# A hybrid mixer block: gates and branch projections token-major, SSD heads in alternating halves, and another lane order at the start

## Chip, cores and metric

One core of one Trainium2 chip. The metric is the device time of one execution in microseconds, median of three runs: 2150.59 (2144.82 to 2153.54). All data are float32; the large matmuls split each operand into two float32r parts (hi and lo) and add three products.

## What is computed

One layer of a diffusion transformer over 256 tokens of width 2048. The inputs x and ctx are normed and modulated, projected by a wide w_in, and run through four branches (gated depthwise convolution, SSD scan, Fourier mixing, RWKV-7 scan). Each branch is projected to width 2048, weighted by a sigmoid gate of its own, and summed; then come w_o, a residual and a squared-ReLU MLP. Cut to what the change touches:

```python
def gated_merge(gate_pre, branches, w_o):
    gates = jax.nn.sigmoid(gate_pre).reshape(b, l, N_BRANCH, D_MODEL)   # gate_pre = h @ w_in[:, 5976:], 4 x 2048 columns
    m = gates[:, :, 0] * branches[0]
    for i in range(1, N_BRANCH):
        m = m + gates[:, :, i] * branches[i]                            # branches[i] = features @ out_i
    return m @ w_o

# ssd_scan, for each of 12 heads (64 wide), two directions, chunks of 128:
y_diag = jnp.einsum('bgrcls,bcsgrp->bclgrp', CB[:, :, None] * L, xd)
y_off = jnp.einsum('bclgn,bcgrpn->bclgrp', Cc, states[:, :-1]) * jnp.exp(a_cs)[..., None]
# modulation: mod = silu(c) @ mod_w + mod_b  (2048 x 12288), split into sh1, sc1, g1, sh2, sc2, g2
# conformer branch: a depthwise convolution of 31 taps over 512 channels
```

## The kernel before

The kernel is written in a tile framework that orders each engine's instructions by a simulated timeline; a number handed to `high_priority` moves a piece of work forward or back in that order. The big matmuls are the main stream. Beside them run lanes: generators that the main stream advances by `step(us)`. Each `next` of a lane emits a few instructions and yields its own estimate; a lane's rate says how much of its estimate it may emit for each microsecond that the main stream claims, and its offs is its priority.

Stages in order. `startup` loads x and ctx, computes the modulation columns it needs from mod_w (`modblock`, 64 loads of 512 KB in buffers "mw", MW of them; its matmuls are 32 wide and go to four 32-partition groups in turn), and runs the first w_in columns (`startcols`). `mid1` and `mid2` run the other columns of w_in in blocks of 512. Behind mid1's first blocks start the lane `rwkv` (RATE_RWKV, ROFF; its pieces a, A, b, c are weighted by WT, its buffers "x2" are XB) and `mod_lane` (rates MR), which computes the other four modulation vectors on VectorE: a load "rm" of 128x512 of mod_w, MB = 3 in flight, and a multiply-add into "macc" (line 1455). Both `mw` and `rm` loads are issued by SyncE (SP), whose queue is in order. `mid2` goes through the conv, Fourier and SSD columns and then the sixteen gate blocks (loop `for b in range(16)`). The lane `taps` (RATE_TAPS, TOFF) does the 31-tap convolution on VectorE (line 1180) in tiles "vp" and "cv" of the pool "mo", which lives through the whole kernel. When the RWKV pieces are far enough, `mid2` starts the lane `ssd` (RATE_SIDE, SOFF), and when RWKV is done, `fft` and `conv` (RATE_CONV, COFF).

Every weight unit of 2 x 128 x 512 is loaded (`unit`, line 155), cast to hi on ScalarE (line 166) and its rest taken to lo on VectorE (line 167), for each half of 128x512. `mm3` (lines 178 to 180) issues the three products. `block` is feature-major: the weights are the stationary operand, 128 columns at a time, the 256 tokens of h are the moving one, so the output is [feature, token], and one k-tile of 512 columns takes 4 x 3 matmuls of 256 columns. `rowblock` is token-major: 128 tokens of h are stationary, 512 weight columns move, and one k-tile takes 2 x 3 matmuls of 512 columns. The Fourier columns, w_o and the MLP's down projection use `rowblock`; the gate blocks, through `cols`, use `block`.

A gate block ends with a Tanh of each of two PSUM tiles (line 603) into "gs" and a store to DRAM "gd". `outs` goes through the branches in the order rwkv, fft, conv (4 k-tiles each), ssd (6): for each of four blocks of 512 output columns it loads two gate tiles "gt" (line 1530), multiplies, and merges the result into m (lines 1551 to 1554), all feature-major, as `hsplit` and w_o need it.

In `ssd`, each head makes an operand G and an operand Ce in buffers "s2" (S2 = 11) and issues four float32 matmuls of 64 stationary columns (lines 1407 and 1409) into half of a PSUM tile `py`: even heads in partitions 0 to 63, odd ones in 64 to 127. `py` is taken at the even head and read after the odd one. A float32 matmul shows as two records in the trace, a transpose and a float32r matmul as one.

Of the kernel before, what the change touches and what calls it, by code (L numbers as in the profile page):

```python
# [10 lines left out]
P = 128  # L11
OFFS = 100
RATE_RWKV = 1.4
RATE_SIDE = .508
RATE_CONV = .279
AHEAD = 2
S2 = 11
ROFF = 100
SOFF = 100
S1 = 14  # L20
WT = dict(a=1.0, A=.813, b=.999, c=.72)
MR = .26, .26, .109, .244
HB = 5
B4 = 8
COFF = -100
MB = 3
XB = 8
MW = 6
RATE_TAPS = .183
# [6 lines left out]
D = 2048  # L36
# [57 lines left out]
class K:  # L94
# [95 lines left out]
    def run(self):  # L190
        from contextlib import ExitStack
        nc, tc, io = self.nc, self.tc, self.io
        with ExitStack() as es:
# [4 lines left out]
            eh, eg, em, ep, er, ex, ed, ec = [ExitStack() for _ in range(8)]  # L198
# [14 lines left out]
            self.mrate = MR[0]  # L213
            self.rb, self.rx = pool(er, "rb", side="right"), pool(ex, "rx", side="right")
# [3 lines left out]
            ec.close()  # L218
            with ExitStack() as e1:
                self.outs(pool(e1, "o1", side="right"))  # L220
# [46 lines left out]
    def modblock(self, c0, w):  # L267


        nc = self.nc  # L270
        ps = self.psm()[:, :w]
        ke = 1024 // w
        st = max(4, ke)
        for u in range(0, KT, st):
            ws = []
            for k in range(u, u + st, ke):
                raw = self.t(self.sp, "mw", [P, 1024], bufs=MW).rearrange("p (t c) -> p t c", t=ke)
                nc.sync.dma_start(raw, self.wap(self.io["mod_w"][0], k, ke, c0, w))  # L278
# [309 lines left out]
    def mid2(self, prep, er, open_ssd, open_side):  # L588
# [11 lines left out]
        def gate(b):  # L600
            def evac(i, ps):
                o = self.GS()
                nc.scalar.activation(o, ps, AF.Tanh, scale=0.5)
                nc.sync.dma_start(self.g_d[2 * b + i], o)
            return evac
# [8 lines left out]
        for b in range(16):  # L614
            cols(C_G + 512 * b, gate(b))
# [547 lines left out]
    def taps(self):  # L1163
# [4 lines left out]
        for f in range(4):  # L1168
            vp = self.t(self.mo, "vp", [P, 4, 94], bufs=1)
# [3 lines left out]
            cv = self.t(self.mo, "cv", [P, TOK], bufs=1)  # L1173
# [82 lines left out]
    def ssd(self):  # L1256
# [66 lines left out]
        py = None  # L1323
        for hf in range(2):
# [11 lines left out]
            for gl in range(2):  # L1336
# [30 lines left out]
                for hl in range(3):  # L1367
# [33 lines left out]
                    yield 2.5  # L1401
                    if h % 2 == 0:
                        py = self.psm()
                    o = py[64 * (h % 2):64 * (h % 2) + 64, :TOK]
                    xo = (192 * gl + 64 * hl)
                    for i in range(2):
                        nc.tensor.matmul(o, xtk[:, 2 + i, xo:xo + 64], G[:, i], start=i == 0, stop=False)
                    for d in range(2):
                        nc.tensor.matmul(o, S0[:, d, 64 * hl:64 * hl + 64], Ce[:, d], start=False, stop=d == 1)
# [22 lines left out]
    def mod_lane(self):  # L1432
# [4 lines left out]
        for which in (2, 4, 3, 5):  # L1437
# [4 lines left out]
            for j in range(4):  # L1442
                acc = self.t(self.mo, "macc", [P, 512])
                for kt in range(KT):
                    while len(ahead) < MB and todo:
                        w2, j2, k2 = todo.pop(0)
                        raw = self.t(self.mo, "rm", [P, 512], bufs=MB)
                        nc.sync.dma_start(raw, io["mod_w"][0][k2 * P:(k2 + 1) * P, w2 * D + 512 * j2:w2 * D + 512 * j2 + 512])
                        ahead.append(raw)
# [59 lines left out]
    def outs(self, op):  # L1509
# [3 lines left out]
        for n in ("rwkv", "fft", "conv", "ssd"):  # L1513
# [13 lines left out]
            for b in range(4):  # L1527
                gt = [self.t(op, "gt", [P, 512], bufs=4) for _ in range(2)]
                for i in range(2):
                    nc.sync.dma_start(gt[i], self.g_d[(gi * 16 + b * 4) // 2 + i])  # L1530
                acc = [self.t(self.pa, "acc", [P, 512]) for _ in range(2)]
                for u in range(k // 2):
                    wu = self.unit([(self.wap(io[wname][0], 2 * u, 2, 512 * b, 512), 0)], 2, 512)
                    for f in range(4):
                        for i in range(2):
                            kt = 2 * u + i
                            c = (f % 2) * TOK
                            self.mm3(acc[f // 2][:, c:c + TOK], (wu[i][0][:, f * P:f * P + P], wu[i][1][:, f * P:f * P + P]),
                                     F[kt], u == 0 and i == 0 and f % 2 == 0,
                                     u == k // 2 - 1 and i == 1)  # L1540
                    self.step(2.4)
# [6 lines left out]
                for i in range(2):  # L1548
                    m, om = half(self.m[b], i), half(old, i)
                    if first:  # L1550
                        nc.vector.scalar_tensor_tensor(m, gt[i], 1.0, acc[i], op0=ALU.add, op1=ALU.mult)
                    else:
                        nc.vector.scalar_tensor_tensor(gt[i], gt[i], 1.0, acc[i], op0=ALU.add, op1=ALU.mult)
                        (nc.vector if n == "ssd" else nc.gpsimd).tensor_tensor(m, om, gt[i], op=ALU.add)
            first = False
        self.hx = ([], [])
        for b in range(4):
            self.hsplit(self.hx, self.m[b], self.p0)
# [184 lines left out]
```

## Time and profile before

| | |
|---|---|
| median of three runs | 2150.59 us |
| the profiled execution | 2151.65 us, of it a span of 2149.9 |
| TensorE, its records' share of the span | 96% |
| VectorE, ScalarE, GpSimd | 70%, 48%, 12% |
| bytes moved | 450.99 MB, mean 210 GB/s |

The trace is one execution. Times are from the span's start. A matmul's record is longer than the distance to the next one's start, since matmuls are pipelined and their ends are modelled: what one costs in a stream is read from starts.

### The profile page before, as it was taken

Reading aid. Unit: us, or ns where it says so; the run is one execution under the profiler, and the core shown is the slowest. Engines: PE = TensorE matmul, PEld = TensorE weight load, DVE = VectorE, ACT = ScalarE, POOL = GpSimd, SP = SyncE. Lnnn points to the kernel's source line nnn. Section 1 sums busy time; section 2 is a strip of 40 time slices with the busy share of each in tenths; the row PEclk is TensorE's granted clock in tenths of the full one; section 3 lists DMA queues with packets and bytes.
Section 4 is the critical chain, followed back from the end, with each engine's and each line's share of the span. In section 5 each row is a group of like instructions: output and inputs, shape, how many; then the busy total and the mean of one; then the engine's idle time right before and its main releaser. Section 6 shows DMA issues by size and latency. Waiting matters only on the chain.

```text
span 2149.9 us, 39741 instructions
## 1 busy us (share of the span) xinstructions
PE 2058.0 (96%) x14894; PEld 1884.8 (88%) x14894; DVE 1503.0 (70%) x2699; ACT 1022.7 (48%) x1934; POOL 251.9 (12%) x285
## 2 busy tenths in 40 slices
PE   6999999999999999899999999999999999999997
PEld 5758999998989999798888998899998889999886
DVE  5645875679999779587987787565766655555555
ACT  4212443454654554355666645464554444545443
POOL 1001430022131022021221140000000000000001
PEclk9999999999999999899999999999999999999999
DMA  9983636767666765579876677546867666666554
GB/s 337 318 273 106 186 87 203 234 165 219 197 187 201 214 185 167 177 219 299 265 247 197 205 270 263 188 124 184 262 205 271 234 210 185 185 185 192 192 194 157
DMA packets 310828, 450.99 MB, mean 210 GB/s; under 512 B 70969, under 2 KB 116700, under 8 KB 310124
## 3 DMA queue, kind: packets, MB, share of 16 engines
q1 hardware_dynamic: 308716, 441.86, 65.9%
q10 hardware_dynamic: 1472, 6.49, 0.9%
q8 instruction: 117, 1.92, 0.4%
q14 instruction: 75, 0.61, 0.1%
q0 software_dynamic: 448, 0.11, 0.0%
HBM read 424.22 MB, written 24.16 MB: 209 GB/s over the span
## 4 chain that ended last, share of the span: by engine, by line
PE 71%; DVE 11%; DMA 10%; issue 3%; SPq 2%; ACT 1%; POOL 1%; DVEq 0%; ACTq 0%; POOLq 0%
PE acc L180 20%; PE acc L179 20%; PE acc L178 20%; DMA rm<-in_mod_w 3%; DVE lo L167 2%; DMA raw<-in_w_in 2%; PE sm L282 2%; DVE macc L1455 2%; PE sm L1009 1%; DMA t<-scrA 1%; ACT hi L166 1%; DMA scrA<-x 1%; DMA raw<-in_fourier_out 1%; DVE tm L800 1%; SPq L278 1%
## 5 line engine op out<-in xcount | busy, mean ns | idle before, releaser
L167 DVE TENSOR_TENSOR lo<-raw,hi 128x512 fp32r<-128x512 f32 x1096 | 760.8, 712 | 434.4 <-ACT hi L166 414.6
L166 ACT CAST hi<-raw 128x512 fp32r<-128x512 f32 x1096 | 651.6, 617 | 800.0 <-PE acc L179 442.6
L180 PE MATMUL acc<-h,lo 128*128 128x256 f32 x3056 | 861.6, 286 | 16.1 <-DVE lo L167 15.8
L178 PE MATMUL acc<-h,hi 128*128 128x256 f32 x3056 | 865.7, 286 | 7.7 <-ACT hi L166 5.0
L179 PE MATMUL acc<-h,hi 128*128 128x256 f32 x3056 | 864.7, 285 | 1.5 <-DVE h L173 1.5
L180 PEld LDWEIGHTS acc<-h,lo 128*128 128x128 f32 x3056 | 575.2, 190 | 31.0 <-DVE lo L167 21.4
L178 PEld LDWEIGHTS acc<-h,hi 128*128 128x128 f32 x3056 | 578.4, 190 | 27.0 <-issue 11.8
L179 PEld LDWEIGHTS acc<-h,hi 128*128 128x128 f32 x3056 | 580.0, 190 | 16.4 <-issue 13.4
L1455 DVE SCALAR_TENSOR_TENSOR macc<-rm,sct,macc 128x512 f32<-128x512 f32 x240 | 193.1, 805 | 68.4 <-DMA rm<-in_mod_w 66.9
L179 PE MATMUL acc<-lo,uh 128*128 128x512 f32 x512 | 200.1, 391 | 0.0
L180 PE MATMUL acc<-hi,ul 128*128 128x512 f32 x512 | 199.3, 389 | 0.0
L178 PE MATMUL acc<-hi,uh 128*128 128x512 f32 x512 | 179.0, 389 | 0.0
L178 PEld LDWEIGHTS acc<-hi,uh 128*128 128x128 f32 x512 | 96.1, 188 | 19.9
L179 PEld LDWEIGHTS acc<-lo,uh 128*128 128x128 f32 x512 | 96.1, 188 | 19.9 <-DVE lo L167 0.2
L180 PEld LDWEIGHTS acc<-hi,ul 128*128 128x128 f32 x512 | 96.1, 188 | 19.8
L1689 POOL TENSOR_TENSOR yg<-yg,grow 128x512 f32<-128x512 f32 x8 | 10.9, 1368 | 721.5 <-ACT junk L1688 721.5
L179 PE MATMUL acc<-lo,h 128*128 128x512 f32 x160 | 63.9, 399 | 1.6 <-DVE lo L167 1.6
L180 PE MATMUL acc<-hi,h 128*128 128x512 f32 x160 | 63.3, 396 | 0.0
L1180 DVE SCALAR_TENSOR_TENSOR cv<-vp,col,cv 128x256 f32<-128x256 f32 x120 | 62.7, 523 | 0.4
L472 DVE TENSOR_TENSOR ua<-acc,ua 128x512 f32<-128x512 f32 (+1 forms) x50 | 34.0, 687 | 38.9 <-PE acc L180 38.6
L178 PE MATMUL acc<-hi,h 128*128 128x512 f32 x160 | 57.5, 396 | 1.1 <-ACT hi L166 1.1
L282 PE MATMUL sm<-mw,s 128*32 128x256 f32 (+2 forms) x448 | 57.0, 450 | 0.0
(379 smaller groups left out, 2476.7 us busy)
## 6 DMA issues: line engine op xcount, KB each, us to landing
raw<-in_w_in SPq DMA_DIRECT2D x216, 512.0 KB, 4.5
rm<-in_mod_w SPq DMA_DIRECT2D x256, 256.0 KB, 3.6
raw<-in_mlp_up SPq DMA_DIRECT2D x128, 512.0 KB, 3.6
raw<-in_mlp_down SPq DMA_DIRECT2D x128, 512.0 KB, 4.0
mw<-in_mod_w SPq DMA_DIRECT2D x64, 512.0 KB, 6.1
raw<-in_w_o SPq DMA_DIRECT2D x32, 512.0 KB, 3.6
gd<-gs SPq DMA_DIRECT2D x32, 256.0 KB, 4.3
gt<-gd SPq DMA_DIRECT2D x32, 256.0 KB, 3.4
```

Of the source, the lines that this page charges most:

```text
L166: nc.scalar.copy(b, a)
L167: nc.vector.tensor_tensor(c, a, b.bitcast(F32), op=ALU.subtract)
L178: nc.tensor.matmul(out, w[0], x[0], start=st, stop=False, skip_group_check=True)
L179: nc.tensor.matmul(out, w[0], x[1], start=False, stop=False, skip_group_check=True)
L180: nc.tensor.matmul(out, w[1], x[0], start=False, stop=sp, skip_group_check=True)
L278: nc.sync.dma_start(raw, self.wap(self.io["mod_w"][0], k, ke, c0, w))
L282: nc.tensor.matmul(ps[32 * j:32 * j + 32, :], self.s32[:, u + i, :], ws[i], start=u + i < 4, stop=u + i >= KT - 4, skip_group_check=True)
L472: nc.vector.tensor_tensor(ua[:m], ps[:m], ua[:m], op=ALU.add)
L800: nc.vector.tensor_tensor(o, Y[:, :r, u:u + 1].broadcast_to([P, r, n]), U[:, u:u + 1, u + 1:].broadcast_to([P, r, n]), op=ALU.mult)
L1009: nc.tensor.matmul(ch(ps, i), self.tb[n][d][:, i], ch(v, i), start=True, stop=True)
L1180: nc.vector.scalar_tensor_tensor(o, v, w, o, op0=ALU.mult, op1=ALU.add)
L1455: nc.vector.scalar_tensor_tensor(acc, raw, w, acc, op0=ALU.mult, op1=ALU.add)
```

## The change

The gate blocks run through `rowblock`, so gates are stored token-major: [token, column]. The projections of the branches in `outs` do the same, and the merged m is token-major. Because w_o needs m feature-major, a new function `mcols` transposes each block of m on TensorE (eight transposes of 128x128 a block) and splits it from PSUM; blocks 0 to 2 are done one SSD block later, block 3 at the end. In `ssd` an even head keeps its operand pairs, and the odd head issues all eight matmuls, alternating between the two halves of `py`. mod_lane's loads are placed behind the last mod_w load of the startup on their queue. "vp" and "cv" move to a pool "tp" that is open only in the middle. Startup has seven "mw" buffers in place of six, RWKV seven "x2" in place of eight, and rates, weights and priorities of the lanes have other values.

```diff
-RATE_RWKV = 1.4
-RATE_SIDE = .508
-RATE_CONV = .279
+RATE_RWKV = 1.451
+RATE_SIDE = 0.69
+RATE_CONV = 0.28
-ROFF = 100
-SOFF = 100
+ROFF = 68
+SOFF = 30
-WT = dict(a=1.0, A=.813, b=.999, c=.72)
-MR = .26, .26, .109, .244
+WT = {'a': 1.0, 'A': 0.728, 'b': 1.021, 'c': 0.887}
+MR = (0.26, 0.264, 0.109, 0.244)
-COFF = -100
+COFF = -295
-XB = 8
-MW = 6
-RATE_TAPS = .183
+XB = 7
+MW = 7
+RATE_TAPS = 0.348
...
-                nc.sync.dma_start(raw, self.wap(self.io["mod_w"][0], k, ke, c0, w))
+                self.mwl = nc.sync.dma_start(raw, self.wap(self.io["mod_w"][0], k, ke, c0, w))
...
         def gate(b):
-            def evac(i, ps):
+            def evac(t, acc):
                 o = self.GS()
-                nc.scalar.activation(o, ps, AF.Tanh, scale=0.5)
-                nc.sync.dma_start(self.g_d[2 * b + i], o)
-            return evac
+                nc.scalar.activation(o, acc, AF.Tanh, scale=0.5)
+                nc.sync.dma_start(self.g_d[2 * b + t], o)
+            self.rowblock(win, C_G + 512 * b, range(KT), lambda kt: self.h("x", kt), evac)
...
-            vp = self.t(self.mo, "vp", [P, 4, 94], bufs=1)
+            vp = self.t(self.tp, "vp", [P, 4, 94], bufs=1)
-            cv = self.t(self.mo, "cv", [P, TOK], bufs=1)
+            cv = self.t(self.tp, "cv", [P, TOK], bufs=1)
...
+                    xo = (192 * gl + 64 * hl)
+                    terms = [(xtk[:, 2 + i, xo:xo + 64], G[:, i]) for i in range(2)]
+                    terms += [(S0[:, d, 64 * hl:64 * hl + 64], Ce[:, d]) for d in range(2)]
                     if h % 2 == 0:
+                        even = terms
+                    else:
                         py = self.psm()
-                    o = py[64 * (h % 2):64 * (h % 2) + 64, :TOK]
-                    xo = (192 * gl + 64 * hl)
-                    for i in range(2):
-                        nc.tensor.matmul(o, xtk[:, 2 + i, xo:xo + 64], G[:, i], start=i == 0, stop=False)
-                    for d in range(2):
-                        nc.tensor.matmul(o, S0[:, d, 64 * hl:64 * hl + 64], Ce[:, d], start=False, stop=d == 1)
+                        for n in range(4):
+                            for j, (w, v) in enumerate((even[n], terms[n])):
+                                nc.tensor.matmul(py[64 * j:64 * j + 64, :TOK], w, v, start=n == 0, stop=n == 3,
+                                                 skip_group_check=True)
...
-                        nc.sync.dma_start(raw, io["mod_w"][0][k2 * P:(k2 + 1) * P, w2 * D + 512 * j2:w2 * D + 512 * j2 + 512])
+                        with self.tc.issue_after(self.mwl.ins):
+                            nc.sync.dma_start(raw, io["mod_w"][0][k2 * P:(k2 + 1) * P, w2 * D + 512 * j2:w2 * D + 512 * j2 + 512])
...
-                acc = [self.t(self.pa, "acc", [P, 512]) for _ in range(2)]
-                for u in range(k // 2):
-                    wu = self.unit([(self.wap(io[wname][0], 2 * u, 2, 512 * b, 512), 0)], 2, 512)
-                    for f in range(4):
-                        for i in range(2):
-                            kt = 2 * u + i
-                            c = (f % 2) * TOK
-                            self.mm3(acc[f // 2][:, c:c + TOK], (wu[i][0][:, f * P:f * P + P], wu[i][1][:, f * P:f * P + P]),
-                                     F[kt], u == 0 and i == 0 and f % 2 == 0,
-                                     u == k // 2 - 1 and i == 1)
-                    self.step(2.4)
...
+                self.rowblock(io[wname][0], 512 * b, range(k), lambda kt: F[kt], evac)
+                if n == "ssd":
+                    if b == 0:
+                        self.hx = ([], [])
+                    else:
+                        self.mcols(b - 1)
             first = False
-        self.hx = ([], [])
-        for b in range(4):
-            self.hsplit(self.hx, self.m[b], self.p0)
+        self.mcols(3)
+
+    def mcols(self, b):
+        nc = self.nc
+        m = self.m[b].rearrange("p f t -> p (f t)").rearrange("p (t c) -> p t c", t=2)
+        for i in range(0, 4, 2):
+            ps = self.psm()
+            for q in range(2):
+                for t in range(2):
+                    o = q * TOK + t * P
+                    nc.tensor.transpose(ps[:, o:o + P], m[:, t, (i + q) * P:(i + q) * P + P], self.cs("ident"))
+            self.hsplit(self.hx, ps.rearrange("p (q c) -> p q c", q=2), self.p0, i)
```

## Rows read from the trace of the kernel before

**Rows 1.** The page: span, busy time by engine, and the chain's engines.

```profile
span 2149.9 us, 39741 instructions
PE 2058.0 (96%) x14894; PEld 1884.8 (88%) x14894; DVE 1503.0 (70%) x2699; ACT 1022.7 (48%) x1934; POOL 251.9 (12%) x285
...
PE 71%; DVE 11%; DMA 10%; issue 3%; SPq 2%; ACT 1%; POOL 1%; DVEq 0%; ACTq 0%; POOLq 0%
```

**Rows 2.** Busy time by stretch; its last columns: granted clock, DMA share, GB/s.

```profile
25.00:100.00 75.00, 69.95 (x646) 55.03 (x647) 49.08 (x112) 23.00 (x50) 0.13 (x2) 1.00 1.02 357
100.00:230.00 130.00, 127.29 (x877) 96.44 (x876) 71.53 (x132) 27.47 (x44) 11.95 (x25) 0.99 0.55 179
230.00:500.00 270.00, 258.83 (x2100) 251.08 (x2098) 190.33 (x368) 125.56 (x240) 57.81 (x52) 0.98 0.61 176
500.00:720.00 220.00, 210.41 (x1676) 200.65 (x1677) 214.07 (x458) 118.12 (x227) 38.77 (x29) 1.00 0.68 199
720.00:1000.00 280.00, 263.63 (x2082) 253.14 (x2081) 207.53 (x420) 130.64 (x259) 37.40 (x41) 0.96 0.69 209
1000.00:1208.00 208.00, 195.06 (x1470) 178.88 (x1470) 172.18 (x296) 129.58 (x283) 53.85 (x75) 1.00 0.75 235
1208.00:1320.00 112.00, 111.32 (x879) 108.24 (x878) 96.10 (x135) 53.65 (x92) 25.18 (x18) 1.00 0.74 251
1425.00:2150.00 725.00, 713.34 (x4616) 652.60 (x4615) 428.35 (x647) 347.60 (x603) 13.90 (x10) 1.00 0.65 203
```

**Rows 3.** Timeline, TensorE, first and last of 57 consecutive starts, MLP up.

```profile
1439.81 0.28 PE L178 MATMUL acc<-h,hi 128*128 128x256 f32 x1
...
1446.45 0.28 PE L180 MATMUL acc<-h,lo 128*128 128x256 f32 x1
```

**Rows 4.** Timeline, TensorE, 25 lines of MLP down and the next.

```profile
1639.82 0.39 PE L179 MATMUL acc<-lo,uh 128*128 128x512 f32 x1
...
1645.94 0.28 PE L1459 MATMUL sm<-cst,macc 128*128 128x1 f32 x2
```

**Rows 5.** Instructions of tile gs: the gates' evacuations, ns, first and last start.

```profile
L603 ACT ACTIVATE gs<-acc x32: 575/592/607, 665.1 to 1206.2; 128x512 f32<-128x512 f32 x32
```

**Rows 6.** The chain in order of time: twelve transposes of the startup.

```profile
101.60 1.37 PE sm L402 x12
```

**Rows 7.** Timeline, TensorE: one SSD head and the next start.

```profile
1012.60 1.08 PE L1407 MATMUL sm<-s,b 128*64 128x256 f32 x4
1013.52 1.03 PE L1409 MATMUL sm<-s,s 128*64 128x256 f32 x4
1014.47 0.39 PE L180 MATMUL acc<-h,lo 128*128 128x256 f32 x1
```

**Rows 8.** Instructions of line 1407: ns min/median/max, first and last start.

```profile
L1407 PEld LDWEIGHTS sm<-s,b x48: 132/137/137, 1012.6 to 1208.2; 128*64 128x64 f32 x48
L1407 PE MATMUL sm<-s,b x48: 379/379/431, 1012.6 to 1208.4; 128*64 128x256 f32 x48
```

**Rows 9.** Timeline, TensorE: modblock's four 32-wide groups, and the next start.

```profile
41.16 1.07 PE L282 MATMUL sm<-mw,s 128*32 128x256 f32 x16
42.16 0.38 PE L178 MATMUL acc<-h,hi 128*128 128x256 f32 x1
```

**Rows 10.** Instructions of tile rm from 0 to 110 us, ns.

```profile
L1448 SPq DMA_DIRECT2D rm<-in_mod_w x19: 327/429/1884, 25.5 to 90.3; - x19
L1455 DVE SCALAR_TENSOR_TENSOR macc<-rm,sct,macc x15: 740/743/754, 31.7 to 89.6; 128x512 f32<-128x512 f32 x15
```

**Rows 11.** SP's own waits from 20 to 180 us: total us, times, longest.

```profile
SPq L278 <- PE sm L282: 44.6, 27, 4.2
```

**Rows 12.** Busy time by stretch of line 1180 alone: DVE, clock, DMA share, GB/s.

```profile
500.00:720.00 220.00, 62.64 (x120) 1.00 0.68 199
```

More of the change, by code (lines that the diff above doesn't have):

```diff
@@ L197, in run @@
             self.dr = pool(es, "dr", space=DRAM)
-            eh, eg, em, ep, er, ex, ed, ec = [ExitStack() for _ in range(8)]
+            eh, eg, em, ep, er, ex, ed, ec, et = [ExitStack() for _ in range(9)]
             self.mo = pool(es, "mo", side="right")
@@ L213, in run @@
             self.mrate = MR[0]
+            self.tp = pool(et, "tp", side="right")
             self.rb, self.rx = pool(er, "rb", side="right"), pool(ex, "rx", side="right")
@@ L218, in run @@
             ec.close()
+            et.close()
             with ExitStack() as e1:
@@ L614, in mid2 @@
         for b in range(16):
-            cols(C_G + 512 * b, gate(b))
+            gate(b)
             if not ssd and {("A", 3), ("b", 3), ("c", 2)} <= self.rw_done:
@@ L1322, in ssd @@
         neg = self.cst2[:, 256:512].rearrange("p (o d l) -> p o d l", o=1, d=2).broadcast_to([P, 2, 2, P])
-        py = None
+        py = even = None
         for hf in range(2):
@@ L1528, in outs @@
                 gt = [self.t(op, "gt", [P, 512], bufs=4) for _ in range(2)]
-                for i in range(2):
-                    nc.sync.dma_start(gt[i], self.g_d[(gi * 16 + b * 4) // 2 + i])
-                acc = [self.t(self.pa, "acc", [P, 512]) for _ in range(2)]
-                for u in range(k // 2):
-                    wu = self.unit([(self.wap(io[wname][0], 2 * u, 2, 512 * b, 512), 0)], 2, 512)
-                    for f in range(4):
-                        for i in range(2):
-                            kt = 2 * u + i
-                            c = (f % 2) * TOK
-                            self.mm3(acc[f // 2][:, c:c + TOK], (wu[i][0][:, f * P:f * P + P], wu[i][1][:, f * P:f * P + P]),
-                                     F[kt], u == 0 and i == 0 and f % 2 == 0,
-                                     u == k // 2 - 1 and i == 1)
-                    self.step(2.4)
+                for t in range(2):
+                    nc.sync.dma_start(gt[t], self.g_d[2 * (4 * gi + b) + t])
                 if first:
@@ L1547, in outs, with evac @@
                     self.m[b] = self.t(op, "m", [P, 4, TOK])
-                for i in range(2):
-                    m, om = half(self.m[b], i), half(old, i)
+                def evac(t, acc):
+                    m, om = half(self.m[b], t), half(old, t)
                     if first:
-                        nc.vector.scalar_tensor_tensor(m, gt[i], 1.0, acc[i], op0=ALU.add, op1=ALU.mult)
+                        nc.vector.scalar_tensor_tensor(m, gt[t], 1.0, acc, op0=ALU.add, op1=ALU.mult)
                     else:
-                        nc.vector.scalar_tensor_tensor(gt[i], gt[i], 1.0, acc[i], op0=ALU.add, op1=ALU.mult)
-                        (nc.vector if n == "ssd" else nc.gpsimd).tensor_tensor(m, om, gt[i], op=ALU.add)
-            first = False
-        self.hx = ([], [])
-        for b in range(4):
-            self.hsplit(self.hx, self.m[b], self.p0)
+                        nc.vector.scalar_tensor_tensor(gt[t], gt[t], 1.0, acc, op0=ALU.add, op1=ALU.mult)
+                        (nc.vector if n == "ssd" else nc.gpsimd).tensor_tensor(m, om, gt[t], op=ALU.add)
+                self.rowblock(io[wname][0], 512 * b, range(k), lambda kt: F[kt], evac)
[4 more added lines that the diff above has]
+                        self.mcols(b - 1)
+            first = False
+        self.mcols(3)
[5 more added lines that the diff above has]
+            for q in range(2):
+                for t in range(2):
+                    o = q * TOK + t * P
+                    nc.tensor.transpose(ps[:, o:o + P], m[:, t, (i + q) * P:(i + q) * P + P], self.cs("ident"))
+            self.hsplit(self.hx, ps.rearrange("p (q c) -> p q c", q=2), self.p0, i)
     def tail(self):
```

## Prediction

> **What bounds the kernel now.** I read the page first: TensorE (PE) is busy 96% of the span, VectorE (DVE) 70%, and PE holds 71% of the chain that ended last [rows 1]. So this is a PE-bound kernel in which the other engines matter only where they make PE wait, and the question for each edit is how much PE time it takes out and whether PE can use it. The view by stages [rows 2] shows where PE has room. From 25 to 100 us the DMA engines are full (share 1.02, 357 GB/s): the startup is bound by loading. From 100 to 230 us the DMA share is 0.55, so it isn't. The busy share flatters PE there: a matmul's record is 0.28 us long while the next starts 0.12 us later, and 877 records at 0.119 us would fill 104 of the 130 us. From 230 to 1208 us, where the lanes (the RWKV and SSD branches) run between the blocks of the big matmul, PE idles 11, 10, 16 and 13 us in the four stretches, some 50 us of 978. From 500 to 720 us DVE is busy 214 of 220 us, nearly a second bound. From 720 to 1000 us the granted clock is 0.96, that is, some 22 us at 1.2 in place of 2.4 GHz, a loss of 11 us. From 1208 to 1320 us (the output projections) PE is full. From 1425 us on nothing is edited.
>
> **The change part by part.** All is reckoned against the profiled execution's own 2151.65 us; the median of the three runs shown is 1.06 us lower.
>
> *Gates.* Sixteen blocks of 512 columns are computed as 192 matmuls of 256 columns each; token-major they are 96 of 512. What one costs is its distance to the next start, not its record. 57 consecutive starts of the 256 form lie 6.64 us apart from first to last, so 0.1186 us each [rows 3]; 27 records of the 512 form (25 lines, two of them x2) take 6.12 us, 0.2267 each [rows 4]. Two of the one against one of the other: 0.2372 - 0.2267 = 0.0105 us. 16 x 96 = 1536 pairs x 0.0105 = 16.1 us. PE is busy about 95% from 500 to 1208 us, and two of the blocks lie where DVE is full, so I take 14; the ends are 8 (half of it turns into waits) and 16.1. Per unit DVE and ScalarE (ACT) do the same work as before, and the evacuations are the same 32 [rows 5].
>
> A rule speaks against this term. The Trainium skill ("TensorE: Matmul & The Clock Gate", section "Back-to-back issue gap") gives N/2.4 + 2.5 ns for a single gap, so joining two would save only 2.5 ns. By it this term and the next would together be 4.9 us, an estimate from that page, and the whole some 14 us less of a gain. The rows give four times that, and they are of these very shapes, so the rule gets no chance here.
>
> *Output projections.* 18 k-tiles x 4 blocks x 12 matmuls of 256 columns become half as many of 512: 432 pairs x 0.0105 = 4.5 us, all on the path, since PE is full there [rows 2]. Added are 32 transposes of 128x128 (mcols): twelve such took 1.37 us [rows 6], so 32 x 0.114 = 3.7 us. They are on PE in the same full stretch, except the last eight, which wait for the last merge while w_o's first k-tiles are ready; I take 3.7 whole, from 0 to 3.7. The splits behind them move the same elements in eight pieces for four, beside other work: nothing.
>
> *SSD heads.* 24 instructions of 256 columns and 64 wide at each of two lines show as 48 records each. Eight records take 14.47 - 12.60 = 1.87 us, 0.234 each [rows 7]; 96 (one line's 48 are in [rows 8]) are 22.4 us. After the edit, matmuls into the two halves of PSUM's partitions alternate. That such halves run together is seen in the startup, where four 32-wide matmuls of the same 256 columns alternate: 16 records in 1.00 us, 0.0625 each, a quarter of 0.234 [rows 9]. Two wide gives a half: 48 x 0.234 = 11.2 us saved. The stretch has PE busy 94% [rows 2]; I take 10. The lower end is with weight loads (0.137 us [rows 8]) that don't overlap the other half: 48 x 0.371 = 17.8, a saving of 4.6. New waits: the even head's four matmuls stand until the odd head's operands are there, so its G and Ce hold two of eleven buffers longer. If the next head's work starts only behind the pair's matmuls, that is up to 1.87 us six times, 11 us, on the lane. The lane is covered: heads end at 1208 [rows 8], SSD's projection is the fourth, after 12 of 18 k-tiles of the 112 us stretch, and the higher RATE_SIDE puts the lane earlier. A PSUM bank is held shorter. Zero.
>
> A rule of the same page speaks against this too ("The mechanism"): weight loads overlap matmuls in flight only when the row group differs, and the halves share all rows. By it the saving would be the lower end. The startup's rows disagree, since their four groups share all rows too.
>
> *Startup.* mod_lane's rm loads now stand behind the last mod_w load. Nineteen of them, 256 KB each, were issued between 25.5 and 90.3 us [rows 10], inside the stretch that is full of DMA: 4.98 MB / 357 GB/s = 14.0 us of loading. They also leave SyncE's (SP's) in-order queue, where an rm load that waits for its buffer holds up the mw loads. PE can't take up all of 14, as it has its own 0.1186 us a matmul to do; its records fill all but some 10 us from 25 to 100 and all but 26 from 100 to 230 by the count above. I take 8, with the seventh mod_w buffer in it (SP waited 44.6 us for such buffers [rows 11]); ends 0 and 14. The 16 macc steps done early (0.74 us each, 11.9 us of DVE) move behind 175 us. DVE is busy 190 of 270 us from 230 to 500, which hides them; if they fall on the DVE-led end of the startup instead, the startup costs up to 4 us.
>
> *Rates, priorities, XB and the taps' pool.* No row shows these by themselves. Their ends are the idle PE time that a better order could fill (30% of 50 us: -15) and the third rival (+37). I take 0, nearest to the stretches where PE is at 94 to 96% now.
>
> Sum: -14 - 4.5 + 3.7 - 10 - 8 = -32.8. 2151.65 - 32.8 = 2118.9, and as a median some 1 us less: **2118 us**. With every term at its own end at once this likeliest case would span 2105 to 2137.
>
> **The rivals.**
> *More comes.* The startup gives the whole 14, the heads 11.2, the gates 16.1 (9.3 more), and the new order fills a third of the idle time and lost clock from 720 to 1000 us (16 + 11 us, so 9): 2118 - 18 = 2100. For it: PE is the bound nearly everywhere. Against: the idle time there hangs on serial chains that the edits don't shorten.
>
> *The lanes keep the time.* From 230 to 1208 us PE's savings (24 us) become waits, because the RWKV and SSD chains set the length; left are the projections (-0.8), the startup and a quarter of the lanes' part: -0.8 - 8 - 6 = -15, so 2136, between 2130 and 2146. For it: DVE is full from 500 to 720. Against: PE idles only 5% there.
>
> *Slower: DVE becomes the bound.* RATE_TAPS nearly doubles and RATE_SIDE rises by 36%. The taps took 62.6 us of DVE between 500 and 720 us [rows 12]; the rest of DVE there is 214.1 - 62.6 = 151.5 of 220, 0.69. Pressed into 0.183/0.348 of the time, 116 us, the taps alone ask 0.54: together 1.23, so 0.23 x 116 = 27 us of waits for the lo splits. The SSD part, pressed likewise where DVE is at 172 of 208 us, may add as much as 10 us. 2118 + 37 = 2155, slower than before. It decides when the demand passes 1. Against: the taps are low-priority filler already; at the old rate they would have spread over far more than 220 us (their steps hold 48 us, at 0.183 that is 262 us of step time, 13.6 gate blocks of 8 x 2.4, and a block takes (1206.2 - 665.1)/15 = 36 us [rows 5]: 490 us).
>
> *It doesn't do what it says.* The two halves run one after the other: the saving of 10 shrinks to 4.6 or 0, 2123 to 2128, inside the range.
>
> **How the numbers follow.** The likeliest 0.55, more 0.18, lanes 0.17, DVE 0.07, halves apart 0.03. The range runs from 2094 (the second case with all 15 of the order's gain in place of 9) to 2147 (the lanes' end and the DVE case with four fifths of its waits). A measurement of this kernel tells about 0.5% from no change, 10.8 us, so faster is below 2139.8: the likeliest, more, halves apart and a third of the lanes' case, 0.82; no change: most of the rest of the lanes' case, 0.10; slower: the DVE case and what is left, 0.08.
>
> **What would show it.** Gate blocks with 512-column records 0.227 us apart; L1407 and L1409's successors in pairs of starts a few ns apart, 16 records in some 1.9 us; no rm load ahead of the last mw load, and the end of the startup (the first block of mid1) 8 us earlier than 230; the stretch of projections about 1 us shorter. DVE at full with longer waits for lo between 500 and 650 would show the third rival; gate blocks as long as before the second. I am wrong if the first rm loads, now 150 us later, come to hold up DVE, or if XB = 7 stretches the RWKV lane past the gates.

## The result and the profile after

The changed kernel takes 2162.55 us (median of 7 runs, 2160.25 to 2164.26); the kernel before takes 2144.82 beside it (7 runs). The ratio is 1.0067 [1.0048, 1.0086]: slower, where 2118 was forecast. (A ratio here is taken over all runs of both kernels side by side, with its 95% interval; it is not the quotient of the two medians. The median of before lies between 2144.8 and 2151.0 us from one set of runs to the next, so differences of kernels from different sets are good to a few us.) The profiled execution of after has a span of 2161.9 us, 12.0 more than before's.

The view by stretch, in the columns of [rows 2]:

```profile
25.00:100.00 75.00, 72.83 (x678) 57.33 (x678) 42.13 (x106) 25.02 (x55) 0.13 (x2) 0.95 0.88 303
100.00:230.00 130.00, 125.75 (x922) 101.43 (x922) 87.85 (x157) 32.37 (x51) 18.33 (x31) 0.99 0.68 226
...
500.00:720.00 220.00, 211.21 (x1424) 189.08 (x1423) 206.60 (x439) 117.24 (x229) 39.79 (x31) 0.99 0.68 198
720.00:1000.00 280.00, 268.00 (x1457) 225.17 (x1456) 204.35 (x405) 138.17 (x269) 33.42 (x41) 0.98 0.67 199
1000.00:1208.00 208.00, 196.44 (x851) 149.54 (x849) 181.74 (x293) 121.94 (x250) 50.97 (x63) 0.98 0.84 275
1208.00:1320.00 112.00, 82.74 (x335) 58.79 (x334) 81.95 (x137) 48.95 (x105) 28.30 (x31) 0.85 0.49 149
```

The last line is the one to see. From 1208 to 1320 us PE was full before (111.32 of 112, clock 1.00 [rows 2]); now it is busy for 82.74, its records are 335 for 879 (a wide matmul stands for two narrow ones, so this alone would leave about half), and the granted clock is 0.85. Two groups of lines tell what moved. The first is the gates' evacuations, the second the SSD heads' matmuls (first and last start at the end of the times):

```profile
L606 ACT ACTIVATE gs<-acc x32: 587/598/607, 644.6 to 1146.6; 128x512 f32<-128x512 f32 x32
```

```profile
L1415 PE MATMUL sm<-s,b x48: 379/430/689, 1044.7 to 1269.4; 128*64 128x256 f32 x48
```

The gates end 60 us earlier than in [rows 5] (1147 for 1206), and the heads 61 us later than in [rows 8] (1269 for 1208). Before, they ended together, and every wait of the SSD lane had gate work beside it. Now the gates are used up first, the projections of the three other branches follow, and then PE has only the lane. PE's four largest waits from 1200 to 1300 us (total us, times, longest):

```profile
PE sm L1415 <- DVE s L1397: 10.1, 2, 6.6
PE sm L1347 <- DVE s L1256: 9.7, 1, 9.7
PE acc L179 <- DVE lo L167: 7.2, 5, 3.3
PE acc L178 <- ACT s L172: 3.9, 1, 3.9
```

In before the same stretch has waits of 0.7 us in all. PE's timeline there shows the lane by itself:

```profile
1246.93 1.11 PE L1415 MATMUL sm<-s,b 128*64 128x256 f32 x2
1247.97 1.65 PE L1367 MATMUL sm<-s,s 128*128 128x192 f32 x4
1256.23 1.54 PE L1415 MATMUL sm<-s,b 128*64 128x256 f32 x5 [6.61 <-DVE s L1397]
1257.15 0.63 PE L1415 MATMUL sm<-s,s 128*64 128x256 f32 x1
```

A head's operands come from DVE 6.61 us after PE ran dry, and the records that follow are 0.63 us long where a head's median was 0.379 [rows 8]: after the waits the granted clock of a stretch is 0.50, 1.2 GHz:

```profile
1256.00:1260.00 4.00, 3.67 (x14) 1.70 (x14) 0.76 (x4) 2.31 (x7) 0.87 (x2) 0.50 0.21 61
```

The rest of the loss is behind the middle, in code that nobody edited. From the start of the MLP to the end the trace takes 739.7 us, 730.8 before. The up-projection takes as long as before (185.5 + 182.2 us, before 186.3 + 182.2); the down-projection takes 180.8 + 179.0 us, before 176.1 + 173.9. Its timeline, the first of 20 consecutive starts and the one behind the twentieth:

```profile
1641.20 0.39 PE L180 MATMUL acc<-hi,ul 128*128 128x512 f32 x1
...
1645.87 0.39 PE L179 MATMUL acc<-lo,uh 128*128 128x512 f32 x1
```

4.67 us / 20 = 0.2335 us each, where [rows 4] have 0.2267.

### The profile page after: what moved, and what is told of

It reads as the page before. It is cut to its first block, busy times and chain, and to the rows that moved or that the text cites. A ratio compares the mean times of both kernels' runs of the same rounds, so it can differ in the third digit from the quotient of the medians.

```text
span 2161.9 us, 35772 instructions
## 1 busy us (share of the span) xinstructions
PE 2057.4 (95%) x12958; PEld 1780.0 (82%) x12958; DVE 1506.3 (70%) x2703; ACT 1023.9 (47%) x1938; POOL 245.9 (11%) x285
## 4 chain that ended last, share of the span: by engine, by line
PE 75%; DVE 12%; DMA 6%; issue 4%; ACT 1%; SPq 1%; POOL 1%; DVEq 0%; ACTq 0%; POOLq 0%
PE acc L179 21%; PE acc L178 21%; PE acc L180 21%; DVE lo L167 3%; PE sm L284 2%; PE sm L1012 2%; DMA raw<-in_w_in 2%; DVE macc L1463 1%; DMA s<-crow 1%; DVE cv L1183 1%; DMA rm<-in_mod_w 1%; DVE tm L803 1%; DVE t L805 1%; DMA t<-scrA 1%; SPq L280 1%
## 5 line engine op out<-in xcount | busy, mean ns | idle before, releaser
L180 PE MATMUL acc<-h,lo 128*128 128x256 f32 x2032 | 573.3, 284 | 5.9 <-DVE lo L167 5.9
L179 PE MATMUL acc<-h,hi 128*128 128x256 f32 x2032 | 573.2, 283 | 1.9 <-DVE h L173 1.9
L178 PE MATMUL acc<-h,hi 128*128 128x256 f32 (+1 forms) x2032 | 573.1, 284 | 1.5 <-ACT h L172 1.4
L180 PEld LDWEIGHTS acc<-h,lo 128*128 128x128 f32 x2032 | 383.2, 189 | 15.1 <-issue 7.8
L178 PEld LDWEIGHTS acc<-h,hi 128*128 128x128 f32 (+1 forms) x2032 | 382.6, 189 | 12.7 <-issue 9.5
L179 PEld LDWEIGHTS acc<-h,hi 128*128 128x128 f32 x2032 | 383.7, 189 | 10.9 <-issue 7.4
L179 PE MATMUL acc<-lo,h 128*128 128x512 f32 x672 | 272.8, 407 | 8.9 <-DVE lo L167 8.8
L180 PE MATMUL acc<-hi,h 128*128 128x512 f32 x672 | 268.6, 402 | 0.0
L178 PE MATMUL acc<-hi,h 128*128 128x512 f32 x672 | 256.9, 404 | 4.7 <-ACT hi L166 4.7
L179 PEld LDWEIGHTS acc<-lo,h 128*128 128x128 f32 x672 | 127.6, 190 | 43.2 <-DVE lo L167 13.5
L178 PEld LDWEIGHTS acc<-hi,h 128*128 128x128 f32 x672 | 127.1, 190 | 35.1 <-ACT hi L166 6.2
L180 PEld LDWEIGHTS acc<-hi,h 128*128 128x128 f32 x672 | 127.6, 190 | 28.2 <-issue 0.7
```

What stands on the lines that cost most here:

```text
L178: nc.tensor.matmul(out, w[0], x[0], start=st, stop=False, skip_group_check=True)
L179: nc.tensor.matmul(out, w[0], x[1], start=False, stop=False, skip_group_check=True)
L180: nc.tensor.matmul(out, w[1], x[0], start=False, stop=sp, skip_group_check=True)
```

## The experiments

Two things had to be explained: why the lanes are late, and why MLP down is slower. Empty PE below is what is left of 1150 to 1320 us when each matmul that starts there is taken at the median spacing of its kind. Counted with the kinds told apart in another way it comes out up to 2 us different. Gate work left is the number of gate matmuls still to start when the RWKV lane's last matmul (line 1090 of before) starts, of 1536, two narrow ones counted as one. All of it is counted from PE's starts in the traces.

| kernel | us | against before | last gate | heads | gate work left | empty PE |
|---|---|---|---|---|---|---|
| before | 2144.8 to 2151.0 | 1 | 1206 | 1013 to 1208 | 777 | 6 |
| after | 2162.55 | 1.0067 | 1147 | 1045 to 1271 | 404 | 50 |
| token_only | 2177.58 | 1.0141 | 1161 | 1085 to 1298 | 492 | 62 |
| gates_cut | 2139.21 | 0.9959 | 1187 | 1011 to 1206 | 756 | 4 |
| h_aligned | 2131.99 | 0.9937 | 1137 | 1036 to 1260 | 404 | 48 |
| cut_lo | 2127.35 | 0.9886 | 1170 | 1004 to 1234 | 642 | 14 |
| cut_hi | 2116.99 | 0.9845 | 1152 | 1015 to 1234 | 505 | 20 |
| cut_all | 2113.84 | 0.9848 | 1176 | 990 to 1190 | 690 | 1 |

**up_aligned: the place of MLP down's operands.** "vp" and "cv" take 4 x 94 x 4 + 256 x 4 = 2528 bytes a partition, 39.5 times 64. With them out of the pool "mo", everything allocated behind it moves by half of 64 bytes, among it "uh" and "ul", MLP down's stationary operands. The edit gives back 32 bytes and nothing else:

```diff
             self.mo = pool(es, "mo", side="right")
+            self.mo.tile([P, 8], F32, name="pad32")
```

> The changed kernel with 32 unused bytes at the start of the pool mo, nothing else; the order of instructions is the same. Theory place: moving vp and cv out of mo shifted every tile to the right of it by 2528 bytes, which is 32 over a multiple of 64, and the MLP's uh and ul, the stationary operands of the down projection, now start 32 bytes off a 64-byte line; that is why their matmuls of 512 columns start 0.234 us apart in place of 0.227. It expects 0.227 again, 1536 matmuls x 0.007 = 11 us, so 2162.5 - 11 = 2152. Rival chance or clock: the spacing stays 0.234 and the time 2160 to 2164.

2153.82 us, ratio 1.0033 [1.0013, 1.0054]: 8.7 us less than after by the medians, 7 by the ratios. MLP down, the first of nineteen consecutive starts and the one behind the nineteenth:

```profile
1640.67 0.39 PE L178 MATMUL acc<-hi,uh 128*128 128x512 f32 x1
...
1645.02 0.40 PE L178 MATMUL acc<-hi,uh 128*128 128x512 f32 x1
```

4.35 / 19 = 0.2289 us, from 0.2335. PE starts the same 12958 matmuls in the same order as in after, place by place, and the moving operands, the weights' hi and lo, lie in another pool that the edit doesn't move. From the start of the MLP to the end the trace takes 733.8 us, 739.7 in after and 730.8 in before. So the place is the cause of two thirds of the tail's loss. The last 2 ns to [rows 4] stay open.

**offs_back, rates_back, lane_back: the lanes' numbers.** Made from after: the old priorities (first diff), the old rates and weights (second, with RATE_CONV, WT and MR), and both.

```diff
-ROFF = 68
-SOFF = 30
-COFF = -295
+ROFF = 100
+SOFF = 100
+COFF = -100
```

```diff
-RATE_RWKV = 1.451
-RATE_SIDE = 0.69
-RATE_TAPS = 0.348
+RATE_RWKV = 1.4
+RATE_SIDE = .508
+RATE_TAPS = .183
...
```

> The changed kernel with the lanes' priorities of the kernel before (ROFF and SOFF 100, COFF -100). Theory priority: the lower priorities of RWKV and SSD let the gate blocks run ahead (they end at 1147 us, 60 earlier than before), so the SSD lane is left over and TensorE waits some 40 us for it between 1200 and 1290 us. It expects that idle time to go: 2162 - 35 = 2125 to 2135, the SSD heads done before the last projections need them. Theory hold: the even head's operands, kept until the odd head, slow the SSD lane itself; then the lane ends as late and the time is 2155 to 2165.

> The changed kernel with the lanes' rates and weights of the kernel before (RATE_*, WT, MR), and its own priorities. Theory priority expects the idle time at the SSD projections to stay, 2155 to 2170. Theory rates (the denser taps and SSD lane make VectorE the bound, and so everything behind them late) expects it to go, 2120 to 2135.

> The changed kernel with all lane numbers of the kernel before: rates, weights and priorities; left are the token-major form, the alternating heads, seven mw and x2 buffers, the taps' pool and the late rm loads. Theory priority or rates: 2125 to 2140. Theory hold, or the token-major form itself: 2155 to 2170.

2166.87 (1.0101 [1.0079, 1.0123]), 2178.76 (1.0159 [1.0141, 1.0178]) and 2181.95 us (1.0176 [1.0158, 1.0194]). No old number brings the lanes forward: the gates end at 1145 to 1151 and the heads at 1271 to 1288. The new rates are worth 16 us to the new kernel, and the times of rates_back and lane_back lie above every range that was given for them. So the lanes' numbers aren't why they are late.

**token_only: the token-major form alone.** Before with the new `gate`, the new `outs` and `mcols`, nothing else.

> The kernel before with the token-major gates and projections alone (mcols too), every other line as before. Theory order: with this form the list of TensorE's instructions lets the gate blocks run ahead of the lanes, so gates end about 1150 and TensorE waits at the SSD projections: 2160 to 2180. Theory other parts (XB, late rm loads, held operands make the lanes late): the form by itself gains what its starts say, 1968 pairs x 0.004 to 0.010 us less 4 us of transposes: 2130 to 2142.

2177.58 us, 1.0141 [1.0112, 1.0170]. This is the part that costs: alone it loses about 30 us. When RWKV's last chain matmul starts, 492 gate matmuls are left, not 777. That is an order, not a race: after, up_aligned and h_aligned, which differ in addresses alone, start all 12958 matmuls in the same order, place by place, in traces of 2161.9, 2152.0 and 2128.8 us, and before and h_only do so with 14894. So this is the order in which the queue was made: more gate work stands ahead of each step of the lanes. Its last stretches (1150 to 1208, 1208 to 1320):

```profile
1150.00:1208.00 58.00, 45.65 (x185) 33.67 (x184) 51.04 (x87) 33.77 (x68) 14.77 (x29) 0.88 0.75 243
1208.00:1320.00 112.00, 81.57 (x301) 57.81 (x300) 85.03 (x135) 50.58 (x117) 42.17 (x43) 0.82 0.47 147
```

**xb7, heads_only, rm_late: the other parts, each alone in before.**

```diff
-XB = 8
+XB = 7
```

```diff
-                        nc.tensor.matmul(o, xtk[:, 2 + i, xo:xo + 64], G[:, i], start=i == 0, stop=False)
...
+                            for j, (w, v) in enumerate((even[n], terms[n])):
+                                nc.tensor.matmul(py[64 * j:64 * j + 64, :TOK], w, v, start=n == 0, stop=n == 3,
```

```diff
+                        with self.tc.issue_after(self.mwl.ins):
                             nc.sync.dma_start(raw, io["mod_w"][0][k2 * P:(k2 + 1) * P, w2 * D + 512 * j2:w2 * D + 512 * j2 + 512])
```

> The kernel before with seven x2 buffers in place of eight. Theory order expects no change, 2143 to 2150. Theory other parts: the RWKV lane's last chain ends 40 us or more later (955 us before, 1015 after the change) and the time is 2155 or more.

> The kernel before with the alternating heads alone. If the pairs run together and no lane suffers: 9 us of TensorE off, 2136 to 2140. Theory hold: heads end 30 us or more later than 1208 us and the time is 2150 or more.

> The kernel before with mod_lane's loads behind the last mod_w load alone (six mw buffers). The startup ends some 8 to 13 us earlier than 252 us. Theory order: 2133 to 2140. Theory other parts: the macc steps that leave the startup load VectorE later and eat it up, 2143 to 2155.

xb7 2145.31 (0.9989 [0.9971, 1.0007]): no change. heads_only 2142.35 (0.9972 [0.9953, 0.9991]): 6 us gained, for 9 expected; its heads end at 1210 us, so holding the even head's operands doesn't make the lane late. rm_late 2143.40 (0.9980 [0.9964, 0.9997]): 5 us gained, less than theory order gave (2133 to 2140); RWKV's first evacuation (its first copy out of PSUM, at the end of the startup) comes at 243 us, 252 before, so the startup's 9 us arrive only in part. The seventh mw buffer was not run alone.

**gates_cut: the wide matmul, or what comes with it?** token_only, in which each gate matmul of 512 columns is two of 256 on the same stationary block. Accumulators, evacuations, stores and sums stay token-major.

```diff
+        if out.shape[-1] == 512 and self.cut:
+            for a, b, s in ((w[0], x[0], st), (w[0], x[1], False), (w[1], x[0], False)):
+                for c in (0, TOK):
+                    nc.tensor.matmul(out[:, c:c + TOK], a, b[:, c:c + TOK], start=s and c == 0, stop=sp and a is w[1],
+                                     skip_group_check=True)
+            return
```

> Before with only the token-major gates, projections and the transposes that follow them, as in token_only, and each 512-column matmul of the gates cut into two of 256 columns on the same stationary block. Data, accumulators, evacuations and stores are those of token_only; only the matmuls' number and width go back. Theory A (the wide matmul itself lets gate work stand ahead of the lanes in PE's queue): the gates end near 1200 again, RWKV's last chain near 950, the SSD heads near 1215, PE's 64 us of empty time between 1150 and 1320 shrink to under 10, and the time is that of before plus the 3.7 us of transposes, 2146 to 2153. Rival B (the token-major evacuations, stores or sums hold the lanes up): heads until 1285 or later and 2172 to 2180, as token_only.

2139.21 us, 0.9959 [0.9943, 0.9975]: 38 us faster than token_only, by a cut that gives PE more instructions. The order is near before's again (756 left), and the stretch before the SSD projection is full. The heads' matmuls of token_only and of gates_cut, and the stretch in gates_cut:

```profile
L1408 PE MATMUL sm<-s,b x48: 379/379/689, 1085.3 to 1298.0; 128*64 128x256 f32 x48
```

```profile
L1418 PE MATMUL sm<-s,b x48: 379/379/431, 1010.7 to 1205.9; 128*64 128x256 f32 x48
```

```profile
1208.00:1320.00 112.00, 109.43 (x488) 88.13 (x488) 94.51 (x134) 53.12 (x93) 25.28 (x16) 1.00 0.75 254
```

So rival B falls, and the cause is the wide matmul itself, through the order. The framework makes each engine's order ahead of the run by a simulated timeline; that this timeline gives a wide matmul less time than two narrow ones, by more than the chip does, fits both orders, but no run shows its prices, so that step is inferred. That it came out 8 us under before, not 3.7 over, wasn't foreseen. In the two profiled executions, 12.6 us apart, the startup ends 3 us earlier, PE is empty for some 10 us less from 250 to 1150 us, and the wide projections save 4, about what the transposes cost; why the first two, nothing here shows.

**h_aligned and h_only: the place of h.** The stationary operand of the wide gate matmuls is h, which in before and after begins 32 bytes past a multiple of 64. One 32-byte constant moved from behind the h tiles to ahead of them mends that; h_aligned does it to up_aligned, h_only to before.

```diff
     def ht(self, pool, dt):
+        if pool is self.p0:
+            self.epsc(1e-12)
```

> up_aligned with one 32-byte constant of pool p0 allocated ahead of the h tiles, so that they begin at a multiple of 64 bytes as MLP up's hi and lo do. Placement theory: the gates', w_o's and Fourier columns' 512-column matmuls start 0.227 us apart in place of 0.2325; 1536 x 0.0055 = 8.4 us for the gates and 384 x 0.0055 = 2.1 us for w_o. Theory A (the SSD lane sets the end of the middle): the gates' share turns into PE waiting for the lane, and only w_o's and a little more is left, 2148 to 2152. Rival B (PE's own work sets it): the whole 11 us, 2141 to 2144. If the placement isn't what separates 0.227 from 0.2325, the spacing stays and the time with it, 2153.8.

> Before with one edit: a 32-byte constant of pool p0 allocated ahead of the h tiles, so that these begin at a multiple of 64 bytes. If h's placement counts only as the stationary operand of 512-column matmuls: 480 of them x 0.0055 = 2.6 us, 2143 to 2146. If it counts as the moving operand of the 256-column matmuls too (0.1135 in place of 0.1185 us in h_aligned): 3072 of the MLP's first product and some 4900 ahead of it x 0.005, less where PE waits for something else, 2110 to 2130. If the narrow matmuls fall back to 0.118 in part, as in feat_best's MLP: 2130 to 2140.

h_aligned takes 2131.99 us (0.9937 [0.9918, 0.9957]), 22 us less than up_aligned (20 by the ratios) and more than either theory gave; in the traces 9 of it come ahead of the MLP and 14 in it. The wide matmuls with h go from a median of 0.232 to 0.230 us, where 0.227 was foreseen. What was not foreseen is the narrow form. Timeline of MLP up in h_aligned, first and last of 57 starts, as in [rows 3]:

```profile
1439.33 0.28 PE L178 MATMUL acc<-h,hi 128*128 128x256 f32 x1
...
1445.67 0.28 PE L180 MATMUL acc<-h,lo 128*128 128x256 f32 x1
```

6.34 us for 6.64: 0.1132 a matmul, not 0.1186. MLP up falls from 186.0 + 182.2 to 179.6 + 174.0 us. But h's place isn't all of it: h_only took 2146.54 us (0.9975 [0.9957, 0.9993]), its MLP up 184.2 + 180.8, with medians of 0.117 and 0.118 and whole stretches at 0.114. cut_lo and cut_hi below share every address of these operands and one MLP, and its second half runs at 0.118 in the one trace and 0.113 in the other. No trace with h at the old place shows 0.113 as a median of any 100 us. The place allows it; what else decides stays open.

**cut_all, cut_lo, cut_hi: which blocks need narrow matmuls.** h_aligned with the cut of gates_cut in all sixteen gate blocks, in blocks 0 to 7 (the diff), in blocks 8 to 15.

```diff
+            self.cut = b < 8
             gate(b)
+            self.cut = False
```

> h_aligned with the gates' 512-column matmuls cut into two of 256, everything else of the change kept. Theory A: the lanes are covered again (heads until about 1215, under 10 us of empty PE between 1150 and 1320): before less 6 us (heads), less 5 to 13 us (startup), less 2 us (w_o), plus 3.7 us (transposes) gives 2125 to 2138. Rival B: the lanes stay late and the gates cost 15 us more, 2155 to 2170.

> cut_all with only gate blocks 0 to 7 cut into 256-column matmuls; blocks 8 to 15 stay 512 wide. Theory A (what counts is how much gate work is queued ahead of the lanes while RWKV's chain still runs, which is beside blocks 0 to 9): RWKV's last chain ends within 15 us of cut_all's 962, the heads near 1210, and half of the gates cost 768 x 0.006 = 5 us less: 2108 to 2116. Rival B (every wide block costs the same share of the lost cover): half way between h_aligned's 2132.0 and cut_all's 2113.8, 2119 to 2126, and the same as cut_hi.

> cut_all with only gate blocks 8 to 15 cut; blocks 0 to 7 stay 512 wide. Theory A: RWKV's last chain is late, as in h_aligned (about 1000), but the SSD heads have narrow gates beside them; PE waits some 15 to 25 us before the SSD projection: 2119 to 2130, above cut_lo. Rival B: the same as cut_lo, 2119 to 2126.

cut_all takes 2113.84 us (0.9848 [0.9831, 0.9865]) and beats both kernels. It is 11 us below theory A's range, which had no term for the MLP: that takes 720.1 us in its trace, 730.8 in before. PE is full before the SSD projection:

```profile
1208.00:1320.00 112.00, 111.17 (x496) 89.93 (x496) 90.72 (x126) 50.36 (x90) 25.95 (x16) 1.00 0.77 262
```

cut_hi takes 2116.99 (0.9845 [0.9810, 0.9880]), cut_lo 2127.35 (0.9886 [0.9845, 0.9927]). Theory A had cut_lo ahead at 2108 to 2116, and that failed. Which of the two is faster isn't shown: their intervals overlap, and so do their runs (2122.57 to 2135.13 for cut_lo, 2113.06 to 2125.78 for cut_hi). cut_lo does bring RWKV's last chain forward, as expected (642 left, not 404), and its empty PE falls to 14 us; but from 850 to 900 us PE stands empty for 15 us, as in before (16) and cut_all (14), where cut_hi and h_aligned have 5 and 7. So the lateness can be mended in good part at either end, while with wide matmuls in the first blocks PE also waits less for the RWKV lane's operands from 850 to 900 us (9.5 us at line 1024 in cut_lo, 0.5 in cut_hi). The two traces differ by 10 us up to the MLP (it starts at 1399.4 and 1389.6) and by 8 in the MLP, which is the open spacing of above. How far the first 10 are due to the place of the cut, one trace of each can't settle.

**feat_best: the old form with the parts that gained.** Before with heads_only, rm_late and h's new place.

> Before with the parts that gained alone: alternating heads (-6 us), the lane's rm loads behind the last mod_w load (-5 us), and the h tiles at a multiple of 64 bytes (w_o and Fourier columns, 480 matmuls x 0.0055 = 2.6 us). If the three add up: before less 13 us, 2130 to 2136. If the gains overlap (the heads' gain needs the earlier start, or the lane's later loads end up late for the outs): 2137 to 2143.

2129.25 us, 0.9922 [0.9907, 0.9938]. The gains add up (18 us for 13, which is at the edge of the interval). cut_all is 15 us faster still, so token-major gates aren't the loss: the order that came with their wide matmuls was. Of the 15, 6 lie in the MLP's spacing (720.1 us for 726.0); cut_all has the new lane numbers too, and the rest isn't taken apart.

## Why the prediction was wrong

**The step that failed** is the one word "Zero" behind "The lane is covered". It took the SSD lane's old end at 1208 us [rows 8] as if it were the lane's own, when it was the end of a queue that lane and gates share. The sum shortened the gates and left the lane's place untouched, so the wait for the lane ahead of the SSD projection stood at nothing; but when the wide form replaces the narrow, the planner lays the whole queue out anew. PE's work was saved where the lanes had it for cover, and some 43 us more of empty PE came ahead of the SSD projection (50 for 6). The second rival, that the lanes keep the time, named the place but stopped at "savings become waits", 2136. It had no way for the lanes to come out later than before, which is what token_only shows at 30 us.

**Gates, -14.** The size was off. The first and last of fourteen starts in after's gates:

```profile
999.78 0.39 PE L178 MATMUL acc<-hi,h 128*128 128x512 f32 x1
...
1002.81 0.39 PE L179 MATMUL acc<-lo,h 128*128 128x512 f32 x1
```

3.03 / 13 = 0.2331 us, not 0.2267. A pair saves 0.2372 - 0.2331 = 0.0041 us, and 1536 of them 6.3, not 16.1. The row was of the right shape and the wrong operand: [rows 4] are MLP down, with uh stationary, and the same trace of before has w_o, with h stationary, the first of 43 starts and the one behind the last:

```profile
1339.76 0.39 PE L179 MATMUL acc<-lo,h 128*128 128x512 f32 x1
...
1349.79 0.40 PE L178 MATMUL acc<-hi,h 128*128 128x512 f32 x1
```

10.03 / 43 = 0.2333. Its nearer row would have given the answer before the run. It would also have made the rule that the prediction set aside (the Trainium skill, "TensorE: Matmul & The Clock Gate", "Back-to-back issue gap": 2.5 ns for a gap) the nearer one: 4.1 ns measured, 10.5 claimed. The whole gap by its formula, 512/2.4 + 2.5 = 216 ns, does not come out here: the starts show 233.

**Projections, -4.5.** Their wide matmuls have a median of 0.234 us in after, so 432 x 0.003 = 1.4. Here the row was right for most of them: in token_only, whose pools are before's, the 288 of rwkv, fft and conv have a median of 0.227 us and the 144 of ssd 0.235. In after the first have 0.234, in up_aligned 0.230, so the moved pool took that part of the term.

**Transposes, +3.7.** Right: two that follow one another start 0.108 to 0.110 us apart, so 3.5 for 32; 24 of the 32 lie between 1293.3 and 1315.7 us, among the projections, as expected.

**Heads, -10.** Right in kind, and alternating as forecast; the size is nearer 8. A pair in after (its first two records, and the other fourteen):

```profile
1044.70 0.65 PE L1415 MATMUL sm<-s,b 128*64 128x256 f32 x2
1045.28 1.13 PE L1152 MATMUL sm<-c,v 128*128 128x512 f32 x2
...
1053.02 0.86 PE L1415 MATMUL sm<-s,b 128*64 128x256 f32 x5
1053.51 0.38 PE L1415 MATMUL sm<-s,s 128*64 128x256 f32 x1
1053.72 0.38 PE L1415 MATMUL sm<-s,b 128*64 128x256 f32 x1
1053.73 1.24 PE L1415 MATMUL sm<-s,s 128*64 128x256 f32 x7
1054.89 1.98 PE L1152 MATMUL sm<-c,v 128*128 128x512 f32 x4
```

Fourteen records in 1.87 us, as long as eight took before [rows 7]; the two that ran ahead alone took 0.58 to the next start. A pair costs 2.45 for 3.74 and six save 7.7; heads_only gained 6 in the time, with an interval of 2 to 10. The rule of the Trainium skill on weight loads ("TensorE: Matmul & The Clock Gate", "The mechanism") that the prediction set aside would have given 4.6 in PE's time. Halves apart didn't happen.

**Startup, -8.** Right in kind and too small: RWKV's first evacuation comes at 239 us, 252 before (five evacuations, before and after, first and last start at the end of the times):

```profile
L639 ACT COPY gs<-acc x5: 615/632/687, 251.6 to 260.4; 128x256 f32<-128x256 f32 x5
```

```profile
L642 ACT COPY gs<-acc x5: 617/634/696, 239.2 to 246.8; 128x256 f32<-128x256 f32 x5
```

No rm load is issued before 157.6 us, behind the last mod_w load, and from 25 to 100 us the DMA share is 0.88 with 303 GB/s, before 1.02 with 357 [rows 2]. The term was held down by PE's room, some 10 us from 25 to 100 us, and that sum does not come out: 646 records at 0.1186 us would fill all 75 us, and with each matmul at the median spacing of its kind some 28 us are empty.

**Rates, priorities, XB, 0.** XB was right (xb7), and the priorities came close (offs_back: 4 us). The rates didn't: in the new form the new ones are worth 16 us, the lower end of the bound that was given (-15). The third rival didn't come: DVE is busy 206.6 of 220 us from 500 to 720, less than before.

**"From 1425 us on nothing is edited."** True of the code and not of the addresses. 9 us of the loss are there, and no term or bound of the range had it.

Together, in the two profiled executions: startup -13; from there to the MLP 1183 us for 1167, so +16; +9 in the MLP: the 12.0 us of the two spans. The +16 are, about, -14 for gates and heads, +2 for the projections with their transposes, +43 for the empty PE from 1150 to 1320 us, and -17 for empty PE from 250 to 1150 us (51 for 68), where the queue holds more gate work between the lanes' steps: +14 of 16.

## What to carry to other kernels

A main stream that covers lanes is part of the lanes' price: when its instructions change shape, compare where both end in the new queue before counting PE time as saved, and expect a planner's order to move as a whole. Read what a matmul costs from a row with the same stationary operand, not the same shape alone. A tile that moves between pools shifts whatever is allocated behind it; look at where stationary operands begin.

## What the runs showed of the hardware

The place of an operand in SBUF changes a matmul's spacing. MLP down's 512-column matmuls start 0.2335 us apart with uh and ul 32 bytes past a multiple of 64, 0.2289 when 32 bytes of padding put them on one, and 0.2267 in before, where they also lie on one. 256-column matmuls with h moving show 0.1186 us and, with h on a multiple of 64, 0.1132 in some stretches and 0.118 in others.

Matmuls of 64 stationary columns into the two halves of one PSUM tile, alternating, take 1.87 us for 14 records (after) where one half alone took that for 8 (before), with their weight loads over the same 128 rows.

PE starts its matmuls in one fixed order: the 12958 of after, up_aligned and h_aligned come in the same order, place by place, though the traces last 2161.9, 2152.0 and 2128.8 us.

Where PE waits 3 to 10 us at a time for the lane, the granted clock falls to 0.50 (1256 to 1260 us of after), over the whole stretch to 0.85 (after) and 0.82 (token_only), and the SSD matmuls that follow a wait show 0.63 us for 0.379.
